# A chunked recurrence: block inverse from half-size blocks, and a step whose outputs are issued last

## The chip, the core and the metric

The kernel runs on one core of a Trainium2 chip. TensorE (PE) multiplies matrices, VectorE (DVE), ScalarE (ACT) and GpSimd (POOL) do the elementwise work, and each engine takes its instructions from a queue of its own, in order. The metric is the time of one execution on the device in microseconds (us), the median of three runs.

## The reference

A diffusion backbone with two layers over 512 latent and 256 context tokens. Each layer projects its input, runs four token mixers, merges them by gates, and ends in a large expert stage. The change concerns one mixer, the RWKV-7 scan, which per head and direction computes

```
def step(S, inp):
    r, w, k, v, kk, a = inp
    sa = einsum('bhij,bhj->bhi', S, kk)
    S = S * w - sa[..., None] * (kk * a) + v[..., None] * k
    return S, einsum('bhij,bhj->bhi', S, r)
S, ys = lax.scan(step, state0, xs, reverse=reverse)     # forward and backward, 8 heads
```

with a 64 x 64 state per head, forward and backward over all 768 tokens. The outputs of both directions are added, normed per head, given a bonus and gated.

## The kernel before

The scan is done in chunks of 64 tokens: twelve chunks per direction, two heads (a pair) at a time, forward on partitions 0 to 63 and backward on 64 to 127. Each layer has four pairs, one after the other, in `rwkv_pair`. A pair has these parts:

1. Gram blocks G (L709 on PE, L712 on DVE): products of keys and queries inside a chunk.
2. The elimination (L742 and L745, `eliminate`): the diagonal 32 x 32 blocks of G, 24 per quarter of the partitions, are inverted by back substitution on DVE. W holds the blocks, X the inverse. Row u needs one multiplication (L742) and one subtraction (L745). Columns 22 to 31 and 0 to 21 go as two interleaved chains: 104 instructions.
3. The tail of the inverse, from the last L745 to the first L844: six transposes on DVE (L756, L757, four of L761) put X into XT and into TT. Then TensorE makes the off-diagonal block with 32 x 32 matmuls (L764, L767, copies L770 and L771, L774, L777, and copies L779 and L780).
4. The recurrence, twelve steps. A step reads the state (L836), adds the values (L839), applies the inverse (L844), copies the result out of PSUM on ACT (L846) and DVE (L847), makes the new state with L857 and L868. `output` of the step before (L807 and L809, then L818 or L820) and `natural` (two transposes L182 and two copies L792 for a later step) stand between the copies and L857 in program order. In layer 1 the outputs of the first four steps are not needed and are left out.
5. The norm of the pair (L879 to L903), which belongs to the next pair's `others` and is mixed into its elimination.

Beside this runs `gate_lat`: 32 chunks of the latent gates per layer, each 24 matmuls of 512 columns (L176), a cast on ACT (L204), a split on POOL or DVE (L205), and a tanh on ACT (L911). They depend on nothing in the scan and fill TensorE's waits. After the scan comes attention (L1149 to L1191 and on). A scheduler that works at build time sets the order of each engine's queue from the program's order and its own costs; on the chip that order is fixed.

In the profile a float32 matmul on TensorE stands as two MATMUL instructions, so 24 matmuls are x48; those on operands split in two parts (`wH`, `wL`) are one instruction each.

## Time and profile before

| what | us |
|---|---|
| three runs, median (lowest, highest) | 6534.53 (6518.1, 6548.82) |
| the profiled execution, span | 6533.5 |
| scan of layer 0, by the trace | about 578 to 1113 |
| scan of layer 1, by the trace | about 4164 to 4673 |

The span is the time from the first to the last instruction of one profiled execution; it stands 1 us from the median of the runs, so sums made on the trace can be held against the runs as they are. "Busy" of an engine is the union of its instructions' times. PEclk, or the granted clock, is the share of TensorE's full speed that it was given: 1.00 is 2.4 GHz and 0.50 is 1.2 GHz. "Idle before, <- releaser" names what an engine waited for. A row of the windows view gives, for a stretch, its length, each engine's busy time with the number of its instructions in brackets, the granted clock, and the share and rate of the DMA engines.

### The profile page before, as it was taken

The page shows a single profiled execution, that of the slowest core. Times are in us where ns is not written, and L with a number is a line of the kernel's source. Part 1 is how long each engine was busy: PE and PEld are TensorE (multiplying, and loading weights), DVE is VectorE, ACT ScalarE, POOL GpSimd, SP SyncE. Part 2 cuts the span into 40 slices and gives each one's busy share as a digit, 9 for nine tenths or more (in the row PEclk, how much of TensorE's full clock was granted, in tenths as well). Part 3 has the DMA queues.
Part 4 walks back from the last instruction along what each step waited for, and adds up shares of the span by engine and source line. Part 5 has one row for each costly group of instructions (what it writes and reads, how often), then busy time and mean ns, then how long its engine had stood idle before and what let it go on. Part 6 is the DMA issues. An engine that isn't in the chain of part 4 may idle for free.

```text
span 6533.5 us, 95628 instructions
## 1 busy us (share of the span) xinstructions
PE 5912.4 (90%) x35605; PEld 4895.5 (75%) x35605; DVE 4508.9 (69%) x9402; ACT 2371.0 (36%) x4585; POOL 2217.2 (34%) x1721
## 2 busy tenths in 40 slices
PE   8898998999897998889899788798999888999998
PEld 5677665778776886667677566666678788999998
DVE  6535554667698857888888674546456798578887
ACT  3223222444335842222222332222334467433333
POOL 1101222000038846656655211133100168444442
PEclk9998897999998999999999899799899999999999
DMA  4455222031435688888899435422121446888896
GB/s 175 157 192 181 84 85 72 11 87 58 148 109 185 229 280 305 303 305 315 316 334 335 171 107 177 131 93 74 68 64 41 156 148 226 291 292 294 296 331 246
DMA packets 532162, 1220.90 MB, mean 187 GB/s; under 512 B 46321, under 2 KB 249201, under 8 KB 524017
## 3 DMA queue, kind: packets, MB, share of 16 engines
q1 hardware_dynamic: 339728, 718.16, 33.2%
q0 software_dynamic: 111168, 406.63, 17.0%
q10 hardware_dynamic: 80800, 90.00, 4.0%
q8 instruction: 281, 4.60, 0.3%
q14 instruction: 185, 1.51, 0.1%
HBM read 1041.41 MB, written 173.21 MB: 186 GB/s over the span
## 4 chain that ended last, share of the span: by engine, by line
PE 48%; DVE 14%; issue 8%; DMA 8%; POOL 5%; ACT 2%; SPq 0%; ACTq 0%; POOLq 0%; DVEq 0%
PE pu L1538 10%; PE pa L1789 7%; PE po L1101 4%; POOL row L1008 3%; PE pl L176 3%; PE pm L176 3%; DMA row<-in_peer_v,gix 3%; PE pw L1070 3%; PE ptp L182 2%; PE pv L1789 2%; PE pn L499 2%; DMA row<-in_peer_v 2%; PE pg L1465 2%; DMA row<-in_peer_u,gix 2%; PE pw L176 1%
## 5 line engine op out<-in xcount | busy, mean ns | idle before, releaser
L1538 PE MATMUL pu<-HX,wH 128*128 128x512 f32 (+2 forms) x4608 | 1327.4, 371 | 11.5 <-ACT wH L1524 6.0
L1538 PEld LDWEIGHTS pu<-HX,wH 128*128 128x128 f32 x4608 | 855.9, 194 | 115.1 <-ACT ga L1777 7.0
L1538 PE MATMUL pu<-HX,wL 128*128 128x512 f32 (+2 forms) x2304 | 848.3, 368 | 41.6 <-POOL wL L1526 36.1
L1008 POOL DMA_INDIRECT row<-in_peer_u,gix x384 | 495.3, 1290 | 513.9 <-DVE row L1648 281.1
L1008 POOL DMA_INDIRECT row<-in_peer_v,gix x384 | 495.5, 1290 | 454.6 <-DVE accn L1657 237.9
L1630 ACT CAST wH<-row 128x1024 fp32r<-128x1024 f32 x384 | 401.9, 1047 | 609.2 <-DMA row<-in_peer_v 286.6
L1789 PE MATMUL pa<-CL,wH 128*128 128x512 f32 (+1 forms) x1536 | 566.5, 369 | 26.0 <-DVE CL L1769 25.8
L1789 PE MATMUL pa<-CH,wH 128*128 128x512 f32 (+1 forms) x1536 | 563.7, 367 | 21.5 <-ACT CH L1764 21.4
L1648 DVE SCALAR_TENSOR_TENSOR row<-row,hn 128x1024 f32<-128x1024 f32 x384 | 504.4, 1323 | 99.0 <-DMA row<-in_peer_u,gix 96.8
L1789 PE MATMUL pa<-CH,wL 128*128 128x512 f32 (+1 forms) x1536 | 562.3, 366 | 0.0
L1657 DVE SCALAR_TENSOR_TENSOR accn<-row,gcw,accn 128x1024 f32<-128x1024 f32 x381 | 519.3, 1374 | 61.4 <-DMA row<-in_peer_v,gix 60.8
L1646 DVE TENSOR_TENSOR wL<-row,wH 128x1024 fp32r<-128x1024 f32 x384 | 478.3, 1246 | 119.4 <-ACT wH L1630 118.6
L1538 PEld LDWEIGHTS pu<-HX,wL 128*128 128x128 f32 x2304 | 445.4, 193 | 100.9 <-POOL wL L1526 42.7
L204 ACT CAST wH<-wr 128x1024 fp32r<-128x1024 f32 (+1 forms) x222 | 231.0, 1043 | 574.9 <-PE pl L176 188.4
L980 POOL TENSOR_TENSOR lnst<-lnst,mhalf 128x4 f32<-128x4 f32 (+3 forms) x8 | 9.4, 1180 | 1183.1 <-DVE lnst L979 1183.1
L176 PE MATMUL pl<-X,wH 128*128 128x512 f32 x1024 | 403.7, 457 | 3.7 <-DVE qk L585 3.2
L205 POOL TENSOR_TENSOR wL<-wr,wH 128x1024 fp32r<-128x1024 f32 x64 | 214.4, 3355 | 545.4 <-ACT wH L204 278.2
L1449 POOL TENSOR_SCALAR B<-cst,T 128x128 f32<-128x128 f32 x330 | 383.4, 1170 | 33.6 <-PE pg L1465 20.7
L1789 PEld LDWEIGHTS pa<-CL,wH 128*128 128x128 f32 x1536 | 291.2, 190 | 72.2 <-DVE CL L1769 41.3
L1789 PEld LDWEIGHTS pa<-CH,wH 128*128 128x128 f32 x1536 | 291.2, 190 | 61.4 <-ACT CH L1764 29.1
L205 DVE TENSOR_TENSOR wL<-wr,wH 128x1024 fp32r<-128x1024 f32 (+1 forms) x158 | 191.3, 1213 | 189.3 <-ACT wH L204 188.1
L1764 ACT CAST CH<-ga 128x512 fp32r<-128x512 f32 (+1 forms) x256 | 145.0, 566 | 467.6 <-DVE ga L1761 349.3
(400 smaller groups left out, 13619.4 us busy)
## 6 DMA issues: line engine op xcount, KB each, us to landing
row<-in_peer_v SPq DMA_DIRECT2D x256, 512.0 KB
wr<-in_uT SPq DMA_DIRECT2D x128, 512.0 KB
row<-in_uT SPq DMA_DIRECT2D x128, 512.0 KB
wr<-in_ada_w SPq DMA_DIRECT2D x96, 512.0 KB
wr<-in_w_gate SPq DMA_DIRECT2D x96, 512.0 KB
gdr<-gall SPq DMA_DIRECT2D x32, 1024.0 KB
Gt<-gdr SPq DMA_DIRECT2D x32, 1024.0 KB
gdr<-big SPq DMA_DIRECT2D x24, 1024.0 KB
```

Of the source, the lines that this page charges most:

```text
L176: pe.matmul(o, lw, rw[:, lo:hi], start=(k == 0 and a == 0), stop=(k == nk - 1 and a == 2))
L204: ac.copy(H, raw)
L205: lsplit[0] = (split or ve).tensor_tensor(L, raw, H.bitcast(F32), op=OP.subtract)
L1008: gp.indirect_dma_start(out=rows, out_offset=None, in_=tab, in_offset=bass.IndirectOffsetOnAxis(ap=ix, axis=0))
L1101: pe.matmul(o[r0:r0 + 64, o0:o0 + P], vx(kb), pt[:, j * P:(j + 1) * P], start=(j == 0), stop=(j == nk - 1))
L1449: (gp if e == "gp" else ve).tensor_scalar(B[:, j, :], iota, T3[:, 1, t_ + j:t_ + j + 1], T3[:, 2, t_ + j:t_ + j + 1], op0=OP.is_equal, op1 ...
L1538: pe.matmul(pw[:, :hi - lo], w[:, k, :], x[:, k, :], start=(k == 0 and i == 0), stop=(k == DC - 1 and i == 2))
L1630: ac.copy(H, ready[nx[1]])
L1646: ve.tensor_tensor(L, raw, H.bitcast(F32), op=OP.subtract)
L1648: ve.scalar_tensor_tensor(raw, raw, 1.0, hn[y], op0=OP.mult, op1=OP.mult, accum_out=acts[y][:, j:j + 1])
L1657: ve.scalar_tensor_tensor(accn[y], raw, gcw[y][:, j:j + 1], accn[y], op0=OP.mult, op1=OP.add)
L1789: pe.matmul(pv[:, :TD], w[:, ds], x, start=(k == 0 and i == 0 and (fresh or s == 0)), stop=(k == 1 and i == 2 and (fresh or s == NS - 1)))
```

## The change

Four things are changed, all inside `rwkv_pair` and its constants.

- The elimination works on the two 16 x 16 diagonal blocks of each 32 x 32 block at once (`blocks` is a view of both). It has 15 rows and 30 instructions.
- The missing 16 x 16 corner is made on TensorE. `Bm` is the corner of the matrix, masked on POOL. X is transposed whole, twice, into Ta and Tb. 96 matmuls give `pz`, DVE makes `Zp` from it (identity minus `pz`), 48 matmuls give `px` (copied to XT on ACT), 96 give `pt32` (copied to TT by DVE and ACT). Then the old off-diagonal part follows (before L764 to L780, now L790 to L806).
- In `output` all matmuls that read the state go first and those that read G after them, with the direction as the inner loop.
- In a step, the state update stands before `output` and `natural` instead of behind them.

```
-SPLIT = 22
+                    Bm = ft("Bm")[:, :NP * 32].rearrange("p (n t) -> p n t", t=32)
+                    gp.tensor_tensor(Bm, NDb[:, :NP, :], m16.unsqueeze(1).to_broadcast([P, NP, 32]), op=OP.mult)
...
-                    cols = [eliminate(SPLIT, 32), eliminate(0, SPLIT)]
...
+                    def blocks(t, r0, r1, c0, c1):
+                        return bass.AP(tensor=t.tensor, offset=t.offset + r0 * 32 + c0,
+                                       ap=[list(t.ap[0]), [16 * 33, 2], [32, r1 - r0], [1, c1 - c0]])
+                    for u in range(15, 0, -1):
+                        n = 16 - u
+                        tv = rv.tile([P, 128], F32, name=nm("tmp"), tag="invt", bufs=2)[:, :2 * u * n].rearrange(...)
+                        ve.tensor_tensor(tv, blocks(W, 0, u, u, u + 1).to_broadcast([P, 2, u, n]),
+                                         blocks(X, u, u + 1, u, 16).to_broadcast([P, 2, u, n]), op=OP.mult)
+                        xs = blocks(X, 0, u, u, 16)
+                        ve.tensor_tensor(xs, xs, tv, op=OP.subtract)
...
-                    ve.transpose(XT[0:32].rearrange("p n r -> p r n"), X[0:32])
-                    ve.transpose(XT[96:128].rearrange("p n r -> p r n"), X[96:128].rearrange("p s t -> p t s"))
-                    for d, q in ((0, 1), (1, 0), (0, 0), (1, 1)):
...
-                        ve.transpose(tt[p0:p0 + 32, :, q * 32:q * 32 + 32].rearrange("p n t -> p t n"), src)
+                    ve.transpose(Ta.rearrange("p n r -> p r n"), X)
+                    ve.transpose(Tb.rearrange("p n r -> p r n"), X.rearrange("p s t -> p t s"))
+                    T0, T0T = (Tb, Ta), (Ta, Tb)
+                    quads = [(d, q, d * 64 + q * 32) for q in range(2) for d in range(2)]
+                    pz = wide()
+                    for p in range(NP):
+                        for d, q, p0 in quads:
+                            pe.matmul(pz[p0:p0 + 32, p * 32:p * 32 + 32], Bm[p0:p0 + 32, p, :], T0T[d][p0:p0 + 32, p, :],
+                                      start=True, stop=True)
+                    ve.scalar_tensor_tensor(Zp, pz[:, :T]..., -1.0, id32..., op0=OP.mult, op1=OP.add)
+                    px = wide()
+                    for p in range(NP):
+                        for d, q, p0 in (quads[0], quads[3]):
+                            pe.matmul(px[p0:p0 + 32, p * 32:p * 32 + 32], T0[d][p0:p0 + 32, p, :], Zp[p0:p0 + 32, p, :],
...
+                    pt32 = wide()
+                    for p in range(NP):
+                        for d, q, p0 in quads:
+                            pe.matmul(pt32[p0:p0 + 32, p * 32:p * 32 + 32], Zp[p0:p0 + 32, p, :], T0[d][p0:p0 + 32, p, :],
...
-                        for d in range(2):
-                            for h in range(2):
...
-                                if S is not None:
-                                    pe.matmul(o, AR[d](c)[h * 64:h * 64 + 64, 64:128], ...
-                                pe.matmul(o, G[d][:, h, c, 64:128], UV[d](c)[:, h * 64:h * 64 + 64],
+                        outs = [(d, h, cd[d], py[real[d] % 2 * 64:real[d] % 2 * 64 + 64, h, 0:64])
+                                for h in range(2) for d in range(2)]
+                        if S is not None:
+                            for d, h, c, o in outs:
+                                pe.matmul(o, AR[d](c)[h * 64:h * 64 + 64, 64:128], ...
+                        for d, h, c, o in outs:
+                            pe.matmul(o, G[d][:, h, c, 64:128], UV[d](c)[:, h * 64:h * 64 + 64],
...
-                        if late is not None:
-                            output(*late)
-                        if s + NAT - 1 < NCH - 1:
-                            nats[s + NAT - 1] = natural(s + NAT - 1)
                         if s < NCH - 1:
                             nat = nats.pop(s)
...
+                        if late is not None:
+                            output(*late)
+                        if s + NAT - 1 < NCH - 1:
+                            nats[s + NAT - 1] = natural(s + NAT - 1)
```

The queues that the scheduler makes of it differ as follows. Lines of the changed kernel are three higher near the helpers (L176 becomes L179, L182 becomes L185) and 25 higher after the scan's steps.

On DVE, the end of the first pair's elimination in layer 0 and what follows it, before:

```order
L742 TENSOR_TENSOR tmp_5011<-W_4803,X_4734 128x30
L745 TENSOR_TENSOR X_4734<-X_4734,tmp_5011 128x3x10
L742 TENSOR_TENSOR tmp_5014<-W_4803,X_4734 128x20
L745 TENSOR_TENSOR X_4734<-X_4734,tmp_5014 128x2x10
L742 TENSOR_TENSOR tmp_5017<-W_4803,X_4734 128x10
L745 TENSOR_TENSOR X_4734<-X_4734,tmp_5017 128x10
L756 STREAM_TRANSPOSE XT_5020<-X_4734 32x32x32
L757 STREAM_TRANSPOSE XT_5020<-X_4734 32x32x32
L761 STREAM_TRANSPOSE TT<-X_4734 32x32x32 x4
L780 TENSOR_SCALAR TT<-pw_5079 32x24x32
```

The same place on DVE now; L750 and L753 are the elimination, L769 makes Zp from PSUM, L785 copies the inverse to TT:

```order
L750 TENSOR_TENSOR tmp_4902<-W_4805,X_4734 128x78
L753 TENSOR_TENSOR X_4734<-X_4734,tmp_4902 128x2x3x13
L750 TENSOR_TENSOR tmp_4905<-W_4805,X_4734 128x56
L753 TENSOR_TENSOR X_4734<-X_4734,tmp_4905 128x2x2x14
L750 TENSOR_TENSOR tmp_4908<-W_4805,X_4734 128x30
L753 TENSOR_TENSOR X_4734<-X_4734,tmp_4908 128x2x15
L758 STREAM_TRANSPOSE Ta_4911<-X_4734 128x32x32
L759 STREAM_TRANSPOSE Tb_4912<-X_4734 128x32x32
L769 SCALAR_TENSOR_TENSOR Zp_5012<-pw_4915,cst 128x768
L785 COPY TT<-pw_5066 32x24x32 x2
L806 TENSOR_SCALAR TT<-pw_5219 32x24x32
```

Four transposes are gone, and three instructions that read PSUM stand where one stood. On PE the tail now has, in this order: 1 matmul L766, 5 gate matmuls, 95 matmuls L766, 6 gate matmuls, 48 of L774, 96 of L782, 24 of L790, 24 of L793, 12 gate matmuls, 24 of L800, 24 of L803 (first pair; with the four ahead of L869 it has 27 gate matmuls, the other tails 24 to 27, where 10 to 13 stood). Between the matmuls L732 (now L737) and the tail's first, 48 gate matmuls stand in the first pair, where 97 stood, and 44 to 50 in the others, where 97 to 103 stood.

On PE, one step of the second pair in layer 0 before, from one reading of the state to the new state:

```order
L836 MATMUL pw_7443<-S_7436,AR_6068 64x64 x2
L836 MATMUL pw_7443<-S_7436,AR_6071 64x64 x2
L176 MATMUL pl<-X_112,wL_9274 128x512
L807 MATMUL pw_7495<-S_7436,AR_6068 64x64
L176 MATMUL pl<-X_112,wH_9273 128x512
L844 MATMUL pc<-w0s_7448,TT 64x64 x4
L176 MATMUL pl<-X_113,wH_9273 128x512
L176 MATMUL pl<-X_112,wL_9274 128x512
L857 MATMUL pw_7443<-UV_6076,nat_7352 64x64 x2
L857 MATMUL pw_7443<-UV_6077,nat_7352 64x64 x2
L809 MATMUL pw_7495<-UV_6076,G_6583 64x64
L807 MATMUL pw_7495<-S_7436,AR_6068 64x64
```

The same kind of step now; L861 reads the state, L831 and L834 are the output, L869 applies the inverse, L878 makes the new state:

```order
L861 MATMUL pw_7826<-S_7808,AR_6348 64x64 x2
L861 MATMUL pw_7826<-S_7808,AR_6351 64x64 x2
L831 MATMUL pw_7852<-S_7765,AR_6348 64x64
L831 MATMUL pw_7852<-S_7765,AR_6351 64x64
L831 MATMUL pw_7852<-S_7765,AR_6348 64x64
L831 MATMUL pw_7852<-S_7765,AR_6351 64x64
L834 MATMUL pw_7852<-UV_6356,G_6863 64x64
L834 MATMUL pw_7852<-UV_6357,G_6864 64x64
L834 MATMUL pw_7852<-UV_6356,G_6863 64x64
L869 MATMUL pc<-w0s_7831,TT 64x64 x4
L834 MATMUL pw_7852<-UV_6357,G_6864 64x64
```

The eight output matmuls, which alternated L809, L807, L809, L807 behind the state update, now stand as four and four between L861 and L869.

On PE, the end of the last pair in layer 0 before; L901 belongs to the pair's gate, L182 to its norm, L176 with YH and L1168 to attention:

```order
L809 MATMUL pw_8416<-UV_7014,G_7521 64x64
L901 MATMUL pw_8450<-lg,g_4700 128x256
L182 MATMUL pw_8438<-cst,Yn_7941 128x128 x6
L176 MATMUL pm<-YH_9589,wH_11018 128x384
L176 MATMUL pm<-YL_9590,wH_11018 128x384
L1168 MATMUL pw<-uq,dTl 128x512 x2
```

The same place now, around the norm's transposes:

```order
L179 MATMUL pl<-X_113,wH_9901 128x512
L179 MATMUL pl<-X_112,wL_9902 128x512
L179 MATMUL pl<-X_112,wH_9901 128x512
L179 MATMUL pl<-X_113,wH_9901 128x512
L185 MATMUL pw_8998<-cst,Yn_8501 128x128 x6
L179 MATMUL pl<-X_112,wL_9902 128x512
L179 MATMUL pl<-X_112,wH_9901 128x512
```

Behind the last output of layer 0 stand 27 gate matmuls, the six transposes, and 130 more gate matmuls before attention's first; none stood there before. In layer 1 it is 24, four transposes, and 150.

## Rows read from the trace of the kernel before

**Rows 1.** The page's first line.

```profile
span 6533.5 us, 95628 instructions
```

**Rows 2.** Windows over the eight eliminations: the first, and the sum of all eight.

```profile
601.50:630.50 29.00, 22.93 (x94) 17.98 (x90) 28.32 (x104) 5.26 (x8) 17.26 (x4) 0.88 0.28 92
...
sum 262.50, PE 208.76 PEld 161.89 DVE 242.01 ACT 53.85 POOL 144.82; mean PE 26.10 PEld 20.24 DVE 30.25 ACT 6.73 POOL 18.10
```

**Rows 3.** Windows over the eight tails: the third, and the sum of all eight.

```profile
895.00:907.00 12.00, 12.00 (x216) 9.85 (x214) 11.83 (x6) 3.27 (x6) 2.41 (x1) 1.00 0.28 101
...
sum 136.60, PE 123.64 PEld 101.93 DVE 103.00 ACT 29.41 POOL 19.71; mean PE 15.46 PEld 12.74 DVE 12.88 ACT 3.68 POOL 2.46
```

**Rows 4.** Timeline of DVE in the first elimination: start, us, instruction, idle before.

```profile
623.26 0.26 DVE L742 TENSOR_TENSOR tmp<-W,X 128x100 f32<-128x100 f32 x1
...
626.52 0.20 DVE L742 TENSOR_TENSOR tmp<-W,X 128x40 f32<-128x40 f32 x1
...
627.23 2.42 DVE L745 TENSOR_TENSOR X<-X,tmp 128x30 f32<-128x30 f32 x1
```

**Rows 5.** Groups by line on DVE: transposes; reading PSUM.

```profile
L722 DVE STREAM_TRANSPOSE W<-ND 64x1024 f32<-64x1024 f32 x8 | 15.9, 1990 | 14.3 <-ACT ND L718 14.3
...
L780 DVE TENSOR_SCALAR TT<-pw 32x768 f32<-32x768 f32 x8 | 7.7, 963 | 30.9 <-ACT TT L779 30.9
```

**Rows 6.** Timeline of PE in the first tail, and behind the second pair's Gram blocks.

```profile
632.56 1.70 PE L764 MATMUL pw<-XT,G 32*32 32x32 f32 x48 [0.97 <-DVE XT L756]
...
641.75 2.60 PE L774 MATMUL pw<-TT,Z 32*32 32x32 f32 x45
...
644.20 0.24 PE L777 MATMUL pw<-TT,Z 32*32 32x32 f32 x1
...
644.23 0.24 PE L774 MATMUL pw<-TT,Z 32*32 32x32 f32 x1
...
724.11 0.92 PE L732 MATMUL pc<-UV,G 64*64 64x64 f32 x24 [0.70 <-ACT KV L734]
```

**Rows 7.** Timelines: PE in the first elimination, ACT in the second.

```profile
620.99 0.63 PE L176 MATMUL pl<-X,wL 128*128 128x512 f32 x1
...
622.27 0.63 PE L176 MATMUL pl<-X,wL 128*128 128x512 f32 x1
...
728.08 1.05 ACT L204 CAST wH<-wr 128x1024 fp32r<-128x1024 f32 x1 [2.42 <-PE pl L176]
...
733.67 1.05 ACT L204 CAST wH<-wr 128x1024 fp32r<-128x1024 f32 x1 [4.04 <-PE pl L176]
```

**Rows 8.** Timeline of ACT, the copy L846 once per step, layer 0 and layer 1.

```profile
789.16 0.26 ACT L846 COPY UV<-pc 64x128 f32<-64x128 f32 x1 [1.09 <-PE pc L844]
...
840.44 0.26 ACT L846 COPY UV<-pc 64x128 f32<-64x128 f32 x1
...
4494.79 0.26 ACT L846 COPY UV<-pc 64x128 f32<-64x128 f32 x1
...
4501.80 0.26 ACT L846 COPY UV<-pc 64x128 f32<-64x128 f32 x1 [1.90 <-PE pc L844]
```

**Rows 9.** Groups by line on PE over the scan of layer 0.

```profile
L809 PE MATMUL pw<-UV,G 128*64 128x64 f32 x384 | 60.9, 248 | 0.0
L807 PE MATMUL pw<-S,AR 64*64 64x64 f32 x352 | 57.9, 246 | 0.9 <-DVE Yn L820 0.8
...
L857 PE MATMUL pw<-UV,nat 128*64 128x64 f32 x352 | 23.4, 244 | 0.8 <-ACT UV L846 0.8
...
L836 PE MATMUL pw<-S,AR 64*64 64x64 f32 x352 | 16.2, 246 | 0.0
```

**Rows 10.** Timeline of PE at the end of both scans.

```profile
1108.05 1.52 PE L182 MATMUL pw<-cst,Yn 128*128 128x128 f32 x6 [7.25 <-DVE Yn L890]
1118.24 0.69 PE L176 MATMUL pm<-YH,wH 128*128 128x384 f32 x1 [8.67 <-ACT YH L1149]
...
4669.02 1.09 PE L182 MATMUL pw<-cst,Yn 128*128 128x128 f32 x4 [6.49 <-DVE Yn L890]
```

More of the change, by code (lines that the diff above doesn't have):

```diff
@@ L72 @@
 C_HIND = C_SGB + 1
-NC_ = C_HIND + 2
+C_M16 = C_HIND + 2
+C_I32 = C_M16 + 32
+NC_ = C_I32 + 32
 @with_exitstack
@@ L116, in tile_backbone @@
     wmn = cst[:, C_WMN:C_WMN + P]
+    m16 = cst[:, C_M16:C_M16 + 32]
+    id32 = cst[:, C_I32:C_I32 + 32]
     def V(l, off, n=1):
@@ L734, in rwkv_pair @@
                         ac.copy(KV[q // 2][:, q % 2 * 3:q % 2 * 3 + 3], pk)
-                    def eliminate(a, b):
-                        for u in range(b - 1, 0, -1):
-                            lo = max(a, u)
-                            n = b - lo
-                            tv = rv.tile([P, 256], F32, name=nm("tmp"), tag="invt", bufs=2)[:, :u * n].rearrange(
-                                "p (a b) -> p a b", b=n)
-                            ve.tensor_tensor(tv, W[:, :u, u:u + 1].to_broadcast([P, u, n]),
-                                             X[:, u:u + 1, lo:b].to_broadcast([P, u, n]), op=OP.mult)
-                            yield
-                            ve.tensor_tensor(X[:, :u, lo:b], X[:, :u, lo:b], tv, op=OP.subtract)
-                            yield
@@ L748, in rwkv_pair @@
-                    cols = [eliminate(SPLIT, 32), eliminate(0, SPLIT)]
-                    while cols:
-                        for x in list(cols):
-                            if next(x, 0) == 0:
-                                cols.remove(x)
+                    def blocks(t, r0, r1, c0, c1):
[3 more added lines that the diff above has]
+                        n = 16 - u
+                        tv = rv.tile([P, 128], F32, name=nm("tmp"), tag="invt", bufs=2)[:, :2 * u * n].rearrange(
+                            "p (k a b) -> p k a b", k=2, b=n)
+                        ve.tensor_tensor(tv, blocks(W, 0, u, u, u + 1).to_broadcast([P, 2, u, n]),
+                                         blocks(X, u, u + 1, u, 16).to_broadcast([P, 2, u, n]), op=OP.mult)
+                        xs = blocks(X, 0, u, u, 16)
+                        ve.tensor_tensor(xs, xs, tv, op=OP.subtract)
@@ new lines, in rwkv_pair @@
+                    Tb = rv.tile([P, 32, 32], F32, name=nm("Tb"), tag="W", bufs=1)
+                    ve.transpose(Ta.rearrange("p n r -> p r n"), X)
[7 more added lines that the diff above has]
+                                      start=True, stop=True)
@@ new lines, in rwkv_pair @@
+                    Zp = ft("Zp")[:, :NP * 32].rearrange("p (n t) -> p n t", t=32)
+                    ve.scalar_tensor_tensor(Zp, pz[:, :T].rearrange("p (n t) -> p n t", t=32), -1.0,
+                                            id32.unsqueeze(1).to_broadcast([P, NP, 32]), op0=OP.mult, op1=OP.add)
+                    px = wide()
+                    for p in range(NP):
+                        for d, q, p0 in (quads[0], quads[3]):
+                            pe.matmul(px[p0:p0 + 32, p * 32:p * 32 + 32], T0[d][p0:p0 + 32, p, :], Zp[p0:p0 + 32, p, :],
+                                      start=True, stop=True)
@@ new lines, in rwkv_pair @@
+                    XT = ft("XT")[:, :NP * 32].rearrange("p (n t) -> p n t", t=32)
+                    for d, q, p0 in (quads[0], quads[3]):
+                        ac.copy(XT[p0:p0 + 32], px[p0:p0 + 32, :T].rearrange("p (n t) -> p n t", t=32))
+                    pt32 = wide()
+                    for p in range(NP):
+                        for d, q, p0 in quads:
+                            pe.matmul(pt32[p0:p0 + 32, p * 32:p * 32 + 32], Zp[p0:p0 + 32, p, :], T0[d][p0:p0 + 32, p, :],
+                                      start=True, stop=True)
@@ L762, in rwkv_pair @@
+                    for d, q, p0 in (quads[2], quads[1], quads[0], quads[3]):
+                        (ve.tensor_copy if d == q else ac.copy)(
+                            tt[p0:p0 + 32, :NP, q * 32:q * 32 + 32],
+                            pt32[p0:p0 + 32, :T].rearrange("p (n t) -> p n t", t=32))
                     pz = wide()
@@ L1956, in constants @@
     k[:, C_HIND + 1] = i >= 64
+    lo, t32 = i[:, None] % 32 < 16, np.arange(32)[None, :]
+    k[:, C_M16:C_M16 + 32] = np.where(i[:, None] < 64, lo & (t32 >= 16), ~lo & (t32 < 16))
+    k[:, C_I32:C_I32 + 32] = i[:, None] % 32 == t32
     return k
```

13 lines of the change are left out of this document (4 added, 9 removed).

## The prediction, made before the run

> **What bounds the kernel now.** The sum is made on the profiled execution, whose span is 6533.5 us [rows 1], 1 us below the median of the three runs. I read the order of the queues first, then the windows view over the parts of each pair, then the timeline of the engine that each part waits for. In both layers the scan is a chain of dependent work, and TensorE's gate matmuls fill its waits.
>
> Three parts of a pair matter. The elimination takes 262.5 / 8 = 32.8 us [rows 2]; DVE is busy nearly throughout, since each instruction needs the one before it, while TensorE does gates. The tail takes 136.6 / 8 = 17.1 us [rows 3]; it is a relay of DVE, PE and ACT. The third tail had the full clock and took 12.0, so the other seven average 17.8. In the recurrence TensorE is the bound: a step takes (840.44 - 789.16) / 10 = 5.13 us with an output in it, but (4501.80 - 4494.79) / 2 = 3.50 where layer 1 leaves outputs out [rows 8]. That is a natural experiment on one of the edits.
>
> **Elimination.** In the first pair, which holds no norm, the 104 instructions take 29.0 us [rows 2]. Two dependent ones are 0.237 us apart at 30 to 40 elements (627.23 - 626.52 for three), 0.037 above the 0.20 that one takes; at 100 elements one takes 0.26 [rows 4]. The new chain has 30 instructions, all dependent, with 91 elements on average (2u(16 - u), summed over 15 rows, is 1360, twice): 30 x 0.287 = 8.6 us. The norm of the pair before stays in it. It is the difference between the pairs with and without one; if the first pair of layer 1 is like that of layer 0, (262.5 - 58.0) / 6 - 29.0 = 5.1, for six of eight pairs, so 3.8 on average.
>
> Then come stalls against POOL: one subtraction took 2.42 where its like takes 0.19 [rows 4], while POOL ran a split, so 2.2 each. The new stretch has 48 gate matmuls, two chunks, so about two splits, and Bm on POOL just before. I take two stalls, 4.4; the ends are none, and four. The sum is 8.6 + 3.8 + 4.4 = 16.8 for 32.8: 16.0 saved per pair, **-128** over eight. Without stalls it is -163, with four -93.
>
> **Tail.** Six transposes of 2 us become two. Beside the 96 old 32 x 32 matmuls come 240 new ones, three more readings of PSUM on the way, and 13 more gate matmuls queued between them. On one tile of the array an instruction takes 1.70 / 48 = 0.035 at full clock and 2.60 / 45 = 0.058 at half; where L774 and L777 use different rows and columns of the array in turn, they start 0.03 apart at half clock [rows 6]. A float32 matmul is two instructions. So the new matmuls, which go in turns over two or four tiles, cost 0.035 (full) or 0.056 (half) each, and the old ones in runs on one tile 0.071 or 0.115. A gate matmul costs (622.27 - 620.99) / 3 = 0.427 at half and (733.67 - 728.08) / 24 = 0.233 at full clock [rows 7]. A transpose of 1024 elements is 2.0, a reading of 768 elements from PSUM 0.96 [rows 5].
>
> In order, half clock and full: two transposes 4.0, 4.0; pz (96) 5.4, 3.4; then Zp (1.0) against six gate matmuls that stand ahead of L774, so the gates decide, 2.6, 1.4; px (48) 2.7, 1.7; pt32 (96) 5.4, 3.4, which hides px's copies to XT; L790 and L793 5.4, 3.4, which hide the copies to TT; twelve gate matmuls 5.1, 2.8, longer than the copies of Z; L800 and L803 5.4, 3.4; the two last readings 1.9; eight hand-overs of 0.1. That is 38.7 and 26.2. The trace of before has most tails at the low clock, and the new one has more small matmuls, so I take three quarters half clock: about 35, that is 280 for 136.6, **+143**. All full is +73, all half +173.
>
> So the inverse as a whole costs about what it did: what DVE gives up, TensorE and the hand-overs take.
>
> **Recurrence.** Over the scan of layer 0, L807 and L809 keep TensorE for 57.9 / 44 + 60.9 / 48 = 2.6 us per step. L836 and L857, of the same shapes but grouped by shape, take 16.2 / 44 + 23.4 / 44 = 0.9 [rows 9]. The alternation of 64-row and 128-row matmuls is the difference, and the new order groups them. They also move between L861 and L869, where TensorE waits for the sum on DVE anyway. Behind the state update nothing of the output is queued any more; `natural` and the gates are. A new step is then one without output (3.5) and what of the 0.9 the wait does not cover. I take 3.7; the ends are 3.5 and 4.4. Layer 0 has ten such steps per pair, layer 1 seven: 68 x (5.13 - 3.7) = 97. The last output of each pair, outside the steps, saves about 1.1 each, 9. Together **-106**; at 3.5 it is -120, at 4.4 -59.
>
> **The end of the scan.** The gates are TensorE work that does not go away. The new queue has 157 gate matmuls behind layer 0's last output and 174 behind layer 1's, where there were none, and attention queues behind them. At full clock that is 36.6 + 40.5 = 77. TensorE stood idle there for 7.25 + 8.67 and for 6.49 us [rows 10], and the norm runs beside the gates, so 22 of it is hidden: **+55**. From 157 to 174 is seven chunks, and a chunk takes 5.6 us by TensorE's own time [rows 7]. Attention has no comparable waits that could take the rest. Were the queue held up by the casts and splits of each chunk, it would be up to 20 more.
>
> **Sum.** -128 + 143 - 106 + 55 = -36: 6497 us.
>
> The addition to the constants (64 columns, loaded once) and the two more instructions on POOL per pair are put at nothing: POOL is busy 18.1 of 32.8 us in the eliminations [rows 2]. Were Bm late, pz would be too, by at most a split's few us per pair.
>
> **Rivals.**
>
> *The new matmuls do not overlap.* All four tiles of a pz write the same columns of PSUM for different rows of the array, and L774 and L777 overlapped on different columns only. Then 240 matmuls cost 0.115 or 0.071 instead of 0.056 or 0.035: 13 us more per pair at 0.75 half clock, 8 x 13 = 104, that is 6601, slower than before. It decides from about 0.03 us more per matmul, since 69 us turn the forecast into +33. Against it: twelve 64 x 64 matmuls L732, whose row halves alternate and which write one tile in PSUM, went at about 0.03 per instruction, (0.92 less a tail of 0.2) / 24, at full clock [rows 6]. Chance 0.10.
>
> The Trainium skill has this as a rule: "TensorEngine Tiling (Array Packing)", section "Restrictions and Gotchas", says that different row tiles cannot use the same PSUM bank at the same time. By that rule the time would be this rival's; the L732 row speaks against it, with four tiles untested here.
>
> *The tail gets the full clock.* The denser queue would keep TensorE at 1.00 as in the third tail [rows 3]: +73 instead of +143, 6427. Against it: seven of eight tails of before were longer. Chance 0.15.
>
> *The steps do not shrink.* `natural`, the gates and the two hand-overs by way of PSUM become the bound at 4.4: 6544, no change. For it: one PSUM buffer serves outputs and `natural` in turn. Against it: the 3.5 in layer 1. Chance 0.18.
>
> *The change does what it says and the gates hide as before:* the order of the queue excludes it, since attention stands behind them.
>
> **How the numbers follow.** The forecast has 0.57, with a range of its own from 6465 to 6530, from one stall more or less per pair and 0.2 us in a step. The bound for a change that can be told from none is 0.5%, 33 us, so 6502 and 6567. Faster: of the forecast 0.36, and 0.15 of the full clock, 0.51. Same: 0.20 of the forecast and 0.17 of the steps, 0.37. Slower: 0.10 of the first rival, and 0.01 each of the forecast and of the steps, 0.12. The range that holds 8 in 10 takes in the full clock's time partly and the third rival whole: 6435 to 6555.
>
> **What would show it.** In the new profile: first to last L753 near 16 us per pair, with some subtractions of 2 us and more; last L753 to first L869 near 35, the clock at 0.5 in most; matmuls L766 below 0.06 us each; L871 copies 3.6 to 3.8 us apart from the third step; after the last L834, 35 to 40 us of L179 before L1193. It is wrong if L766 takes over 0.1 each, if the L871 copies stay 4.4 or more apart, or if the tail keeps the full clock.

## The result, and the profile after

The changed kernel took 6462.65 us (median of four runs, 6459.97 to 6482.01); the kernel before, run beside it, 6541.67. The ratio is 0.9885 with a 95% interval of 0.986 to 0.9911: faster by about 1.1%, inside the forecast range (6435 to 6555) and 34 us below its point of 6497.

The table adds up the parts of all eight pairs in the profiled executions, by the stretches of the prediction, in us. "Ends" is the time from TensorE's last output matmul to attention's first matmul, both layers added.

| part | before | after | difference | forecast |
|---|---|---|---|---|
| eliminations | 262.6 | 124.0 | -138.6 | -128 |
| tails of the inverse | 136.7 | 258.2 | +121.5 | +143 |
| recurrences | 486.4 | 360.8 | -125.6 | -106 |
| ends | 20.1 + 7.4 | 54.7 + 43.1 | +70.3 | +55 |
| sum | 913.2 | 840.8 | -72.4 | -36 |

The two spans differ by less, 53.3 us. The rest lies between attention of layer 0 and the Gram blocks of layer 1, which took 3063.6 us in this one profiled execution and 3036 to 3054 in those of before and of all nine experiments. It was the slowest of the four runs; the others took 6460 to 6464. Of the executions behind the experiments below one stands apart, of the run with one quarter at a time: it took 19912 us at a granted clock of 0.53, and that run's median counts it while its ratio leaves it out.

The windows over the same parts, of the changed kernel (columns as in [rows 2]): first the eliminations and the tails, each with the first pair and the sum of all eight, then the sum of the recurrences.

```profile
601.70:613.60 11.90, 8.71 (x54) 6.74 (x50) 10.85 (x30) 2.43 (x4) 3.85 (x2) 1.00 0.36 115
...
sum 124.10, PE 93.59 PEld 73.52 DVE 103.70 ACT 31.14 POOL 41.43; mean PE 11.70 PEld 9.19 DVE 12.96 ACT 3.89 POOL 5.18
```

```profile
613.60:645.40 31.80, 25.84 (x699) 21.71 (x700) 7.63 (x6) 7.79 (x10) 3.36 (x3) 0.69 0.09 27
...
sum 258.20, PE 209.53 PEld 174.43 DVE 59.06 ACT 63.70 POOL 27.95; mean PE 26.19 PEld 21.80 DVE 7.38 ACT 7.96 POOL 3.49
```

```profile
sum 360.60, PE 360.60 PEld 239.66 DVE 120.21 ACT 130.76 POOL 128.59; mean PE 45.08 PEld 29.96 DVE 15.03 ACT 16.34 POOL 16.07
```

The rows of before that answer to the first two are [rows 2, 3]; that of the recurrences, not shown yet, is this sum.

```profile
sum 486.70, PE 483.26 PEld 319.94 DVE 125.88 ACT 132.63 POOL 119.60; mean PE 60.41 PEld 39.99 DVE 15.73 ACT 16.58 POOL 14.95
```

Two things are to be seen. In the tail the work has moved: DVE was busy 103 of 136.6 us and is now busy 59 of 258, while TensorE, busy for most of it in both, runs about 700 instructions per tail where it ran 204 to 216. In the recurrence TensorE is busy throughout in both, and it is TensorE's own work that shrank, from 483 to 361 us.

### The profile page after: what moved, and what is told of

Read it like the earlier page. It is cut to its first block, busy times and chain, and to the rows that moved or that the text cites. A ratio compares the mean times of both kernels' runs of the same rounds, so it can differ in the third digit from the quotient of the medians.

```text
span 6480.2 us, 102749 instructions
## 1 busy us (share of the span) xinstructions
PE 5834.9 (90%) x39445; PEld 4859.2 (75%) x39445; DVE 4321.9 (67%) x8802; ACT 2395.2 (37%) x4617; POOL 2167.7 (33%) x1729
## 3 DMA queue, kind: packets, MB, share of 16 engines
q1 hardware_dynamic: 339728, 718.19, 33.7%
## 5 line engine op out<-in xcount | busy, mean ns | idle before, releaser
L179 PE MATMUL pl<-X,wH 128*128 128x512 f32 x1024 | 401.3, 458 | 3.4 <-DVE qk L588 3.0
L208 POOL TENSOR_TENSOR wL<-wr,wH 128x1024 fp32r<-128x1024 f32 x64 | 152.6, 2384 | 622.7 <-ACT wH L207 549.6
```

The source lines that it names most:

```text
L179: pe.matmul(o, lw, rw[:, lo:hi], start=(k == 0 and a == 0), stop=(k == nk - 1 and a == 2))
L208: lsplit[0] = (split or ve).tensor_tensor(L, raw, H.bitcast(F32), op=OP.subtract)
```

## The experiments

All times below are medians, and a ratio is to the kernel before run in the same batch, with its 95% interval. There were four batches (the changed kernel; the next four rows; the four after them; the last), whose medians of the kernel before were 6541.67, 6540.26, 6527.21 and 6545.03; the rows stand here in the order of the text. The parts are those of the table above.

| run | elimination | tail | recurrence | ends | time | ratio |
|---|---|---|---|---|---|---|
| before | 262.6 | 136.7 | 486.4 | 27.5 | | |
| changed | 124.0 | 258.2 | 360.8 | 97.8 | 6462.65 | 0.9885 (0.986 to 0.9911) |
| recurrence alone | 276.6 | 137.1 | 361.9 | 30.6 | 6426.82 | 0.9823 (0.9786 to 0.986) |
| inverse alone | 126.5 | 247.6 | 474.4 | 90.2 | 6560.57 | 1.0039 (1.0022 to 1.0057) |
| grouping alone | 270.5 | 142.0 | 373.2 | 29.5 | 6436.16 | 0.9842 (0.9812 to 0.9873) |
| moving alone | 264.7 | 126.6 | 479.2 | 27.4 | 6532.45 | 0.9999 (0.9981 to 1.0018) |
| one quarter at a time | 119.3 | 332.9 | 357.6 | 108.0 | 6549.31 | 1.0027 (1.0004 to 1.005) |
| seven gate chunks fewer | 124.0 | 252.8 | 363.8 | 29.1 | 6408.26 | 0.9818 (0.9793 to 0.9844) |
| changed, split on DVE | 110.5 | 248.1 | 366.3 | 63.8 | 6411.67 | 0.9828 (0.9799 to 0.9858) |
| old inverse, split on DVE | 232.5 | 121.2 | 372.2 | 27.4 | 6370.33 | 0.9767 (0.9736 to 0.9797) |
| two quarters at a time | 124.2 | 264.3 | 355.8 | 97.8 | 6463.03 | 0.9878 (0.9847 to 0.9908) |

### Which half of the change gains

Theory A takes the rows as they stand: the gain is the recurrence's, and the inverse, with the gates that it leaves over, costs time. Theory B gives the shorter elimination a gain of its own. Inside the recurrence, A1 puts the gain on the grouping of the output matmuls and A2 on the earlier state update.

**The recurrence alone**: the kernel before, with both edits of the step and the old inverse.

```
-                        for d in range(2):              # in output: state and G matmuls in turn
+                        if S is not None:
+                            for d, h, c, o in outs: pe.matmul(o, AR[d](c)...)
+                        for d, h, c, o in outs: pe.matmul(o, G[d]...)
...
-                        if late is not None: output(*late)      # ahead of the state update
+                        if late is not None: output(*late)      # behind it
```

> The kernel before with only the recurrence changed (state update first, outputs behind it and grouped); the old elimination and its tail stay. Theory A (the gain is the recurrence's, and the new inverse gives nothing once the gate matmuls that no longer fit stand behind the scan): the eight recurrences fall from 487 us to about 361 as in the changed kernel, the eliminations stay at 262 and the tails at 137, all gate matmuls but about 20 stay inside the scan, so the time falls by 110 to 125 us, to about 6425, some 40 below the changed kernel. Theory B (both parts pay, the inverse by its shorter chain on DVE): the time falls by only a part of the change's 79 us, 40 to 60, to about 6490.

It took 6426.82 us, 36 less than the changed kernel. The recurrences fell as far as there, and the ends stayed at 30.6. This beats the whole change.

**The inverse alone**: the changed kernel with the old step.

```
-                        for d, h, c, o in outs: pe.matmul(o, G[d]...)
+                        for d in range(2): for h in range(2): ...   # as before, and ahead of the state update
```

> The kernel before with only the inverse changed (16 x 16 elimination and the block step on TensorE); steps and outputs as before. Theory A: eliminations 262 to 124, tails 137 to 258, recurrences unchanged at 487, and about 155 to 175 gate matmuls per layer behind the scan as in the changed kernel, 35 us more at each end: 6535 - 139 + 122 + 70, some 50 us slower than before, about 6590. Theory B: 20 to 40 us faster than before, about 6505.

It took 6560.57 us, 20 more than the 6540.26 beside it, and the interval of the ratio excludes no change. By the parts: eliminations -136, tails +111, recurrences -12, ends +63, together +26. Theory B falls. A had the sign; its size of about +50 was too large.

**Grouping alone and moving alone** split the recurrence's edits.

```
# grouping alone: output() as in the change, its place in the step as before
# moving alone:   output() as before, its place in the step as in the change
```

> The kernel before with only the output's matmuls grouped (all that read the state, then all that read G, direction inside); they stay ahead of the state update, and the inverse stays. Theory A1 (what a step paid was the alternation of 64-row and 128-row matmuls on TensorE, 2.1 us instead of 0.7): steps with an output fall from 5.1 to 3.7 to 4.0 us, the time by 85 to 115 us. Theory A2 (what a step paid was the output standing ahead of the state update): the grouped output takes 0.7 us and still stands in the way, and TensorE's 1.3 us go to waits, so steps stay above 4.6 and the time falls by 0 to 30 us.

> The kernel before with only the state update moved ahead of the output and of the transposes for later steps; the output's matmuls still alternate, and the inverse stays. Theory A1: TensorE needs its 2.1 us for the output in every step wherever it stands, so steps stay near 5 us and the time within 25 us of before. Theory A2: steps with an output fall to 3.7 to 4.2 us and the time by 70 to 110 us.

Grouping gives 6436.16 us, ratio 0.9842, and moving 6532.45, ratio 0.9999: A1. The trace says why. The rows are PE's timeline over an output of the kernel before, then of the changed one, then of moving alone (start, us, instruction).

```profile
797.13 0.33 PE L809 MATMUL pw<-UV,G 128*64 128x64 f32 x2
797.39 0.33 PE L807 MATMUL pw<-S,AR 64*64 64x64 f32 x2
797.64 0.33 PE L809 MATMUL pw<-UV,G 128*64 128x64 f32 x2
```

```profile
780.48 0.34 PE L831 MATMUL pw<-S,AR 64*64 64x64 f32 x8
780.76 0.45 PE L834 MATMUL pw<-UV,G 128*64 128x64 f32 x8
781.14 0.45 PE L869 MATMUL pc<-w0s,TT 64*64 64x64 f32 x8
```

```profile
802.57 0.33 PE L809 MATMUL pw<-UV,G 128*64 128x64 f32 x2
802.83 0.32 PE L807 MATMUL pw<-S,AR 64*64 64x64 f32 x2
803.09 0.45 PE L853 MATMUL pw<-UV,nat 128*64 128x64 f32 x8
803.37 0.28 PE L809 MATMUL pw<-UV,G 128*64 128x64 f32 x2
```

In turns, each float32 matmul (x2) takes 0.26 us to the start of the next. Grouped, four of them (x8) take 0.28 (780.48 to 780.76) and 0.38 (780.76 to 781.14). An output of eight is about 2.1 us in the one order and 0.7 in the other. Over layer 0 of the kernel before, 146 steps from L807 to L809 take 0.255 us in the median and 122 from L809 to L807 0.258. L807 opens an output and L809 adds to it, so the second kind goes on to another output and costs the same; and where a matmul of the same shape follows (L836 or L844 on L807, L857 on L809), also to another tile, it starts 0.01 to 0.06 later in the median. So it is the change of shape that costs, not the shared output. The edit also turned the two inner loops; L836, which kept the heads inside, takes 16.2 / 44 = 0.37 us for four [rows 9], so the inner order is not what gained.

Where only the place is changed, as in the third fence, the state update (L853) gets in between, but the turns still fill TensorE's queue, and TensorE is what a step waits for. The groups by line over the scan of layer 0 say the same: L834 and L831 of the changed kernel against L809 and L807 in [rows 9].

```profile
L834 PE MATMUL pw<-UV,G 128*64 128x64 f32 x384 | 27.0, 236 | 0.0
...
L831 PE MATMUL pw<-S,AR 64*64 64x64 f32 x352 | 17.5, 232 | 0.0
```

They keep TensorE for 44.5 us instead of 118.8, while an instruction's own time is the same (236 and 232 ns against 248 and 246). The mean of one hides it; the union of busy time shows it. With moving alone, L809 stays at 62.2.

The Trainium skill has a rule for this, "TensorEngine Tiling (Array Packing)", section "Tiling Modes", "Key Properties": changing the tiling mode drains TensorE, changing the tile alone does not. These rows agree, and give the price here: 0.26 us from one matmul to the next where the shape changes each time, against 0.07 to 0.10 within a group.

### The new matmuls: do the tiles overlap, and what paces them

**One quarter at a time**: the changed kernel, with the 240 new matmuls of a pair in runs on one quarter of the partitions instead of in turns.

```
-                    for p in range(NP):
-                        for d, q, p0 in quads:
+                    for d, q, p0 in quads:
+                        for p in range(NP):
```

> The changed kernel with the 240 new 32 x 32 matmuls per pair (L766, L774, L782) in another order: all of one quarter of the partitions first, then the next, instead of in turns over the quarters. Nothing else differs. Overlap theory (the trace of the changed kernel has four L766 on four quarters starting within 0.02 us, 0.05 later the next four, at half clock): in runs on one quarter a matmul pays the one-tile interval of before, 0.115 at half and 0.071 at full clock, so each of the 240 costs 0.04 to 0.09 more: 10 to 20 us more per pair, 80 to 160 in all; time near 6540 to 6620, the tails 258 -> 340 to 420, L766 of the first pair 9 to 11 us long instead of 2.1. Rival (the new tail is long because of its hand-overs and of the gate matmuls queued in it, not of its matmuls): the order matters little, tails within 30 us of 258, time below 6500.

It took 6549.31 us, 87 more than the changed kernel by the medians (93 by the ratios), and the tails are 75 longer, 9.3 per pair; the time is at the low end of what the overlap theory gave, the tails (333) fall just short of its 340, and both are far from the rival. The windows over `pz` of the first pair, of the changed kernel and then of this one; but for a gate matmul at the edge there is nothing but L766 on PE in them:

```profile
618.30:618.90 0.60, 0.60 (x45) 0.58 (x48) 0.00 (x0) 0.01 (x1) 0.60 (x2) 0.50 0.00 0
...
619.40:620.40 1.00, 1.00 (x118) 0.96 (x105) 0.00 (x0) 0.00 (x0) 1.00 (x1) 1.00 0.56 199
```

```profile
616.50:618.80 2.30, 2.30 (x44) 2.30 (x45) 1.67 (x1) 0.00 (x0) 0.57 (x1) 0.50 0.00 0
```

A row counts every instruction that overlaps its stretch, also those begun before it, so the pace is taken from the starts. In turns over four quarters, 16 instructions take 0.213 us at a granted clock of 0.50 (618.516 to 618.729), 0.0133 each, and 0.133 at 1.00 (619.402 to 619.535), 0.0083 each. On one quarter the 192 take 9.62 at 0.50 (616.49 to 626.11), 0.050 each. The timeline shows how they lie: four on four quarters start within 0.02 us, the next four 0.06 after the first.

```profile
618.39 0.24 PE L766 MATMUL pw<-Tb,Bm 32*32 32x32 f32 x1
618.40 0.24 PE L766 MATMUL pw<-Ta,Bm 32*32 32x32 f32 x1
618.41 0.24 PE L766 MATMUL pw<-Tb,Bm 32*32 32x32 f32 x1
618.41 0.24 PE L766 MATMUL pw<-Ta,Bm 32*32 32x32 f32 x1
618.45 0.24 PE L766 MATMUL pw<-Tb,Bm 32*32 32x32 f32 x1
```

The four write the same columns of one tile in PSUM, each on partitions of its own. So the first rival of the prediction falls. The Trainium skill, "TensorEngine Tiling (Array Packing)", section "Restrictions and Gotchas", has the rule that would have made it true; the measurement decides against it here.

**Two quarters at a time.** The changed kernel's tails hold a wait that no tail of before has. Two of the waits of PE in the first tail of the changed kernel (waited for, us in total, times, longest):

```profile
PE pw L766 <- DVE Ta L758: 5.3, 1, 5.3
PE pw L782 <- issue: 3.7, 2, 1.9
```

"Issue" is time in which the engine waited for nothing that the profile shows. It is 34.1 us over the eight tails, in 21 holes of up to 2.8 us before L766, L774, L782, L790 or L793, 0 in before, and 0 with one quarter at a time. To see whether the pace of the bursts makes these holes, L766 and L782 took two quarters at a time:

```
-                    for p in range(NP):
-                        for d, q, p0 in quads:
+                    for p, d, q, p0 in [(p,) + t for two in (quads[:2], quads[2:]) for p in range(NP) for t in two]:
```

> The changed kernel with L766 and L782 in turns over two quarters of the partitions at a time (first the two directions of one head, then of the other) instead of over all four. In the changed kernel these matmuls start 0.008 to 0.014 us apart in bursts, and between the bursts TensorE stands idle for 1.2 to 2.8 us with nothing waited for (34 us over the eight tails; none in the kernel before and none in the run that takes one quarter at a time, at 0.05 us). Theory (the bursts run faster than instructions are supplied to TensorE, and the supply sets the pace): at half the density the bursts last longer and the holes shrink by as much, to under 15 us in all; tails and the whole within 20 us of the changed kernel, 6445 to 6485. Rival (the holes belong to these lines whatever their pace, and four tiles at once are a real gain): the holes stay at 25 us or more, and the tails grow by 3 to 5 us per pair, 25 to 40 in all, to about 6490 to 6505.

The holes fell to 12.1 us, the tails grew by 6, and the time was 6463.03: the theory's case. The waits of its first tail:

```profile
PE pw L766 <- DVE Ta L758: 5.3, 1, 5.3
PE pw L782 <- issue: 2.9, 2, 1.6
```

Two quarters run at half the density, 16 instructions in 0.427 us at 0.50, 0.0267 each. Four tiles at once gain nothing over two here; what the faster burst wins, it loses again in the holes.

The trace shows the supply too. A DMA queue of its own brings instructions in packets of 16 KB: 281 in the kernel before and 311 in the changed one, five of them around the first tail. The first row is that queue (packets, MB, share of 16 engines), the second the end of a hole.

```profile
q8 instruction: 5, 0.08, 1.0%
```

```profile
626.37 0.21 PE L782 MATMUL pw<-Tb,Zp 32*32 32x32 f32 x1 [1.92 <-issue]
```

By the packets' own times two of the five landed at 624.99 and 628.72, and L782 went on at 626.37 and 630.10. All 21 holes of the changed kernel's tails end 1.2 to 1.5 us after such a packet landed, and the 11 of the run with two quarters 1.2 to 1.6. In the tails of both, packets start no closer than 3.3 us apart; with one quarter at a time it is 4.1, and there is no hole. So the supply of instructions is what runs dry; no run changed the supply alone.

### The gates behind the scan

**Seven gate chunks fewer**: the changed kernel with chunks 25 to 31 of each layer left out.

```
-                for f in range(32):
-                    gate_lat(f)
+                for f in range(25):
+                    gl = gate_lat(f)
+                for f in range(25, 32):
+                    ac.dma_start(gscr[f][:, :TL], gl)
```

> The changed kernel, with the last 7 of the 32 gate chunks of each layer left out (their scratch rows are filled with the values of chunk 24, so the gates of 7 chunks are wrong): some 170 matmuls of L179 per layer less, those which in the changed kernel stand behind the scan's last output. Theory (the gate matmuls that the shorter elimination no longer covers are paid behind the scan): last output to attention's first matmul falls from 54.7 and 43.1 us to about 20 and 8, and the time falls by about 70 us to about 6392. Rival (these gates hide: attention waits for the norm and for Y anyway, and the time behind the scan is theirs): less than 25 us off, 6440 or more.

The ends fell from 97.8 to 29.1 us, about what they were before (27.5), and the time by 54; by the ratios it is 0.67% with an uncertainty of about 0.36, so 20 to 67 us. In the profile the two scans, with the way to attention, are 39 and 28 us shorter, together 67. The gates behind the scan are paid nearly in full, as the theory has it; how much of the 67 reaches the time, these runs settle only to that interval.

### The stalls against GpSimd

The prediction counted stalls of DVE against POOL's split of the gate weights. In the first elimination of the changed kernel there is one; DVE's timeline, then POOL's:

```profile
601.75 1.31 DVE L750 TENSOR_TENSOR tmp<-W,X 128x30 f32<-128x30 f32 x1
...
606.57 2.37 DVE L753 TENSOR_TENSOR X<-X,tmp 128x126 f32<-128x126 f32 x1
608.98 0.29 DVE L750 TENSOR_TENSOR tmp<-W,X 128x128 f32<-128x128 f32 x1
```

```profile
601.16 1.85 POOL L724 TENSOR_TENSOR Bm<-ND,cst 128x768 f32<-128x768 f32 x1
606.25 2.54 POOL L208 TENSOR_TENSOR wL<-wr,wH 128x1024 fp32r<-128x1024 f32 x1 [3.24 <-ACT wH L207]
```

The first multiplication ends at 603.06, 0.05 after Bm on POOL (601.16 + 1.85). A subtraction whose like takes 0.29 us ends at 608.94, 0.15 after the split on POOL (606.25 + 2.54). The Trainium skill, "SBUF — State Buffer", section "Who interferes with whom", says that a DVE instruction with two inputs in SBUF contends with a GpSimd instruction that reads SBUF, and that whichever is first keeps the shared port for its whole instruction while the other blocks. These rows agree. So do all the others: of the 832 multiplications and subtractions in the eliminations of the kernel before, 28 take over 0.6 us where the rest take at most 0.39, each ends 0.04 to 0.18 us after a split on POOL, and together they are about 59 us longer than their like. In the changed kernel it is 11 of 240 and about 21 us. Two runs put all the splits on DVE, one with each inverse:

```
-                    H, L = wtile(I["w_gate"][l, f], [P, DC, P], split=gp)
+                    H, L = wtile(I["w_gate"][l, f], [P, DC, P], split=ve)
```

> The changed kernel, with the subtraction that splits each gate chunk's weights (L208, 64 in all) on VectorE instead of GpSimd; the queues are ordered anew around it. Theory of stalls (in the first elimination after the change a subtraction of 0.29 us took 2.37 us, ending when GpSimd's split of 2.5 us ended): GpSimd no longer holds VectorE up; 2.1 us per coinciding split go and 1.2 us of VectorE come, so eliminations 124 -> 105 to 115, and the whole some 10 to 50 us faster. Rival (a split in VectorE's in-order queue waits for ScalarE's cast, and holds up what stands behind it): as fast or slower, with VectorE waiting for ScalarE's wH inside eliminations and steps.

> The old inverse with the new recurrence (outputs grouped and moved behind the state update: the run that was fastest so far, 6427 us) and the gates' split on VectorE instead of GpSimd. Theory of stalls: its eliminations (276.6 us, 104 dependent instructions each, at most 3 to 4 stalls of 2.2 us per pair) lose 0.9 us per split: 10 to 40 us faster than 6427. Rival (VectorE is what bounds the old elimination, so 1.2 us of split each is pure addition, and GpSimd's splits mostly fall where VectorE waits): 0 to 40 us slower.

**The changed kernel with the split on DVE** took 6411.67 us, 51 less than the changed kernel by the medians, 37 by the ratios, and 52 by the sums of the parts. DVE's timeline in its first elimination, and the windows over that one and the sum of all eight:

```profile
608.55 0.29 DVE L753 TENSOR_TENSOR X<-X,tmp 128x126 f32<-128x126 f32 x1
608.76 1.22 DVE L208 TENSOR_TENSOR wL<-wr,wH 128x1024 fp32r<-128x1024 f32 x1
609.90 0.28 DVE L750 TENSOR_TENSOR tmp<-W,X 128x120 f32<-128x120 f32 x1
```

```profile
603.50:613.20 9.70, 9.70 (x46) 7.46 (x42) 8.69 (x31) 3.15 (x5) 0.00 (x0) 1.00 0.41 150
...
sum 110.40, PE 98.36 PEld 77.96 DVE 90.20 ACT 37.82 POOL 11.87; mean PE 12.29 PEld 9.75 DVE 11.28 ACT 4.73 POOL 1.48
```

The split takes 1.22 us on DVE and stands once in the chain; the stall of 2.1 is gone. In this run and the next no multiplication or subtraction of the eliminations takes over 0.39 us. The eliminations fell by 13.5, as expected; the tails fell by 10.1, and the recurrences grew by 5.5. But the larger part, 34.0, is in the ends: 113 and 100 gate matmuls stand behind the last output, where 157 and 174 stood. The scheduler, with other costs on DVE, had issued more of them before. That part the theory of stalls does not explain.

**The old inverse with the new recurrence and the split on DVE** took 6370.33 us, the best of all: 2.3% less than before. Against the recurrence alone it is 56 less by the medians, 37 by the ratios, and 53 by the parts. The rival, that the split would be an addition on a busy DVE, falls. The subtractions by line over the scan of layer 0, in the kernel before and in this one:

```profile
L745 DVE TENSOR_TENSOR X<-X,tmp 128x31 f32<-128x31 f32 (+12 forms) x208 | 69.6, 368 | 1.2
```

```profile
L745 DVE TENSOR_TENSOR X<-X,tmp 128x31 f32<-128x31 f32 (+12 forms) x208 | 48.0, 262 | 1.2
L205 DVE TENSOR_TENSOR wL<-wr,wH 128x1024 fp32r<-128x1024 f32 x32 | 39.1, 1221 | 2.7 <-ACT wH L204 1.7 <-PE pl L176 0.3
```

A mean of 368 ns for what takes 262 with GpSimd quiet was stalls all along, 21.6 us in one layer in this line alone. And the 39.1 us of split on DVE cost less than they relieve. Of the 32 splits 18 stand in the layer's four eliminations; over all eight, the time in which DVE is idle there is 232.5 - 219.5 = 13 us, against 276.8 - 242.4 = 34 in the run with the recurrence alone, so part of the splits went into DVE's waits.

The two inverses can now be held against each other twice, with the same recurrence. Without the split on DVE the parts elimination, tail and ends are 480.0 us in the changed kernel and 444.3 with the old inverse, 35.7 less; the medians, of two batches, differ by 35.8. With it they are 422.4 and 381.1, 41.3 less; the medians, of one batch, differ by 41.3. By the ratios it is 40 both times, with an uncertainty of about 30, and in both comparisons every run with the new inverse is slower than every run with the old one. With the new recurrence the new inverse is a loss of about 40 us; with the old recurrence it was 20 to 26.

## Why the prediction was right, and where its sizes were off

The direction, the sign of each of the four terms and the likeliest case held; the forecast was 34 us above the measured time. The order of the terms by size did not hold: the tail was forecast as the largest and is the third. By the parts the gain was twice the forecast (72.4 for 36), since three terms missed to the same side, by 11, 20 and 22 us, and the ends by 15 to the other. By its own steps:

**Elimination** (-128, measured -138.6). The chain of 30 is what it was said to be: in the run with the split on DVE it takes 9.7 us with one split in it, which holds it up by 1.0 (from 608.55 + 0.29 to 609.90, less the usual 0.03), so 8.7 against 8.6. The stalls were over-counted. Two were taken, 4.4 us; the first pair has one of 2.1, and about 1.1 on its first multiplication, which ends with Bm on POOL (601.16 + 1.85). That is 3.2, against 4.4; over all eight pairs it is about 21 us, 2.7 a pair, which is 14 us less than was taken.

**Tail** (+143, measured +121.5). The step that fails is the price of the overlapped matmuls: 0.056 each at half clock was taken from two tiles that take turns, and four tiles run at about 0.027 (twice 0.0133) at half clock and 0.017 at full. `pz` takes 2.1 us in the first pair (618.3 to 620.4), where 5.4 stood. Part of this came back as the holes in L782, which the prediction did not have: `pt32` takes 6.5 (623.7 to 630.2), where 5.4 stood. And the clock was better than three quarters half: the eight tails were granted 0.61 to 0.78, 0.70 in the mean, which is six tenths of the time at half speed. (Three quarters of 38.7 and a quarter of 26.2 make 35.6, not 35, which alone is 5 us over eight pairs.) With six tenths the prediction's own working gives 26.2 + 0.6 x 12.5 = 33.7 per tail, and 32.3 was measured. The rival of the full clock came about in no tail.

**Recurrence** (-106, measured -125.6). In layer 0 the size held: the copies L871 of the second pair, from the second step to the last, are (798.72 - 763.34) / 10 = 3.54 us apart, against the 3.7 taken and the 4.4 of the third rival.

```profile
763.34 0.26 ACT L871 COPY UV<-pc 64x128 f32<-64x128 f32 x1 [1.06 <-PE pc L869]
...
798.72 0.26 ACT L871 COPY UV<-pc 64x128 f32<-64x128 f32 x1 [3.05 <-PE pc L869]
```

Most of the missing 20 is in layer 1, whose recurrences fell by about 61 us, 15.3 per pair, where the steps of the prediction make 7 x 1.43 + 1.1 = 11.1. In its first pair, from the fourth step on, they take (4253.50 - 4226.35) / 8 = 3.39 us, below the 3.5 that was the prediction's lower end:

```profile
4226.35 0.26 ACT L871 COPY UV<-pc 64x128 f32<-64x128 f32 x1 [1.74 <-PE pc L869]
...
4253.50 0.24 ACT L871 COPY UV<-pc 64x128 f32<-64x128 f32 x1
```

Over the four pairs of the layer the seven steps with an output went from 5.02 us to 3.43, which makes 11.1 a pair where 10.0 was taken. Another 1.9 a pair is the time from a pair's first copy to its second, which was not in the sum; it varies from 5 to 9 us in both kernels, and in layer 0 it grew by 0.7 a pair. The rest is not traced to a cause.

The attribution was only half right. The prediction gave the grouping the first place and let the move do the rest; moving alone is worth nothing that can be measured (0.9981 to 1.0018), and with the grouping it adds about 10 us, inside the intervals of the two runs.

**Ends** (+55, measured +70.3). The 36.6 and 40.5 us of gate matmuls came; the 22 of cover did not all. PE's timeline in the changed kernel, layer 0 and then layer 1, against [rows 10], and the windows over both stretches:

```profile
1039.67 1.51 PE L185 MATMUL pw<-cst,Yn 128*128 128x128 f32 x6 [3.64 <-DVE Yn L915]
...
1082.29 0.69 PE L179 MATMUL pm<-YH,wH 128*128 128x384 f32 x1 [8.66 <-ACT YH L1174]
...
4581.55 0.63 PE L185 MATMUL pw<-cst,Yn 128*128 128x128 f32 x4 [1.84 <-DVE Yn L915]
...
4617.02 2.74 PE L1193 MATMUL pw<-uq,dTl 128*128 128x512 f32 x8
```

```profile
1039.00:1084.00 45.00, 35.36 (x139) 28.13 (x140) 5.86 (x6) 11.92 (x15) 10.53 (x6) 0.84 0.50 168
...
4582.00:4617.00 35.00, 35.00 (x152) 28.14 (x151) 2.60 (x3) 10.04 (x13) 12.34 (x6) 1.00 0.52 173
```

The hole of 8.67 us before YH is still there, 8.66. What YH waits for is a DMA that ACT issues, and that issue now stands behind the casts and activations of the last gate chunks in ACT's queue. The last pair's result is stored from 1045.13 on, six chunks follow, and the issue comes at 1077.10; in the kernel before it came 0.42 us behind the store (1112.68 and 1113.10).

```profile
1045.13 0.33 ACTq L928 DMA_DIRECT2D ybscr<-yb  x1
...
1073.48 1.04 ACT L207 CAST wH<-wr 128x1024 fp32r<-128x1024 f32 x1 [4.06 <-PE pl L179]
...
1075.06 0.33 ACTq L937 DMA_DIRECT2D gscr<-glat  x1
1077.10 1.45 ACTq L1173 DMA_DIRECT2D yraw<-ybscr  x3
1081.41 0.83 ACT L1174 CAST YH<-yraw 128x768 fp32r<-128x768 f32 x1 [6.38 <-DMA yraw<-ybscr]
```

So the prediction's "attention queues behind them" was true of ACT as well as of TensorE, and only TensorE's queue had been read. That is read from the order of the rows; no run moved the issue. In this stretch the clock was 0.84 besides. In layer 1 there is no such hole, and 35.7 came where 40.5 less 6.5 was taken.

**As a whole.** The sentence "the inverse as a whole costs about what it did" set 128 against 143 and left its third term, the gates, apart. Together with the gates it is a loss of about 40 us, which the grouping pays for.

## What to carry to other kernels

Before a chain is shortened, ask what ran in its shadow: a shorter elimination hides fewer gates, and what it no longer hides is queued behind the scan, on every engine that handles it. Where a line's busy time over its count is much more than its neighbours' of the same shape, look at what stands between its instructions; grouping by shape was worth more here than the whole new algorithm. And a mean duration well above that of an instruction's like (368 against 262 ns) was a wait on another engine here, and moving that engine's work removed it.

## What the runs showed of the hardware

- Float32 matmuls that alternate between a 64-row and a 128-row shape start 0.26 us apart, whether or not they share an output; in groups of one shape, four take 0.28 to 0.38.
- Four 32 x 32 tiles on different quarters of the partitions, which write the same columns of one tile in PSUM, run at once: 0.0133 us per instruction at a granted clock of 0.50, against 0.0267 on two quarters and 0.050 on one.
- At that pace TensorE stops for up to 2.8 us with no wait in the profile, 34.1 us over eight tails; at half the density 12.1, at one quarter at a time none. Each stop ends 1.2 to 1.6 us after a packet of 16 KB of the instruction queue landed.
- A split of 128 x 1024 took 2.54 us on GpSimd and held a two-input DVE instruction until it ended (28 times in the eliminations of the kernel before); on DVE it takes 1.22.
